# Nineteen 16-column products without a reader, and one of 512 columns fewer, in an encoder layer on one core

## The chip, the core and the metric

The kernel runs on one core of one Trainium2 chip. The core has a matrix engine (TensorE; PE in the profile, PEld for its weight loads), VectorE (DVE), ScalarE (ACT), GpSimd (POOL) and SyncE (SP), each with an instruction queue of its own that is worked off in order. Data lies in SBUF, and products add up in eight banks of PSUM. The metric is the device time of one execution in microseconds, the median of several runs; lower is better.

## The reference

One layer of a bidirectional encoder, 512 tokens of 1024 channels, all in float32:

```
n = rms_norm(h); proj = n @ w_in
h = h + (gate_a * (s5(xa) @ w_proj_a) + gate_b * (sgu(zu, zv) @ w_proj_b)) @ w_out
hn = rms_norm(h); memn = rms_norm(mem)              # mem: 256 tokens
q = hn @ w_q; k = memn @ w_k; v = memn @ w_v        # 4 heads of 256
h = h + softmax(q k^T / 16) v @ w_xo
hn = rms_norm(h)
h = h + (silu(hn @ w_gate) * (hn @ w_up)) @ w_down   # 1024 -> 2816 -> 1024
out = rms_norm(h)
```

## The kernel before, in words

Each float32 operand is split into a high part, which is the value rounded to the matrix engine's fp32r type, and a low part, the rest. One float32 product is then three fp32r products that add up in PSUM: high by high, high by low, low by high. `mm3` (lines 420 to 426) issues these three; `product` (line 1296) does the same for one of the seven products of a Strassen-like scheme, 24 instructions of 256 columns each: two column blocks j, four k, three parts. A weight block is loaded by DMA, and ScalarE (`whi`, line 85) and VectorE (`wlo`, line 86) split it, two blocks ahead of its use.

The stages that matter here come in this order. **Keys**: `feat(w_k, ...)`, four calls over 256 columns, each into two PSUM banks pf of 256 columns, four groups of twelve products; the moving operand is mn, the normalised memory, and transposes (ptr, line 584) of the query input stand between them. **Values**: two calls of `tokm(w_v, ...)`, each into two banks pt of 512 columns. **Queries**: 14 calls of `product` with q tiles qx, qv and qq (256 columns). Then attention and its output product, whose last blocks of rows t = 0 to 3 (pt, 512 columns) each end in an addition to h, a row norm (ACT square, DVE, POOL power) and a scaling into xs (DVE, line 576). `turn_row(t)` turns xs by eight transposes (ptr, line 1722) into the feed-forward input fn.

**Feed-forward entry**: the list LEAD gives (unit, q) of the first sixteen calls of `product`: (0,1), (1,1), (0,2), (2,1), (1,2), (2,2) and so on. The first two read only the first two blocks of rows. **Units**: eleven column blocks of w_gate and w_up, seven products each; the last one (**the last job**) has two parts of the down product (dx, 512 columns) between its products 6, 7, 4 and 3. **Down**: seven products in 512 columns (dx, dq, dv), and the **last products** (line 2072 on): dv in 256 columns for the last block of rows, then the last norm.

What sets the order: the program is written in one order, and a scheduler with a time model of its own moves instructions of an engine against each other as long as data and buffers allow. An instruction given to `in_order` keeps its place in the written order among those given to it; `pinned[0]` switches that on for whole stretches. In `product`, only the first of the 24 instructions is pinned, and only while `pinned[0]` is set: in LEAD from the third call on. Buffers that another engine frees (PSUM banks by `bank` and `aux`) are waited for by semaphore.

At the fourth call of LEAD stands a product without a reader: `idle`, 512 columns (line 1864), into an `aux` bank that nothing reads.

Of the kernel before, what the change touches and what calls it, by code (L numbers as in the profile page):

```python
# [17 lines left out]
P = 128  # L18
# [34 lines left out]
def hybrid_layer_kernel(  # L53
# [8 lines left out]
    nc = tc.nc  # L62
# [31 lines left out]
    pinned, halved = [False], [None]  # L94
    in_order = tc.keep_in_program_order
# [300 lines left out]
    def next_w(*key):  # L396
        i = used_w[0]
        used_w[0] += 1
        assert len(plan[i][0]) == len(key) and plan[i][0][1:] == key[1:] and plan[i][0][0] is key[0]
        for j in range(i, min(i + FAR + 1, len(plan))):  # L400
            begin(j, i)
            if j - 1 >= len(tiles) and j - 1 <= i + SPLITS:
                split_w(j - 1)
        for j in range(len(tiles), min(i + SPLITS + 1, len(plan))):
            split_w(j)
        tile_, tiles[i] = tiles[i], None
        return tile_
# [10 lines left out]
    def split_w(j):  # L418
        tiles.append(plan[j][2]())

    def mm3(ps, a, b, start, stop, free=False, turn=False):

        for i, (x, y) in enumerate(((0, 0), (0, 1), (1, 0))):
            m = nc.tensor.matmul(ps, a[x], b[y], start=start and i == 0, stop=stop and i == 2, skip_group_check=free)  # L424
            if turn:
                in_order(m)
# [38 lines left out]
    def tokm(w, c0, act, nk, evac, ntok=NT, last=2, kpt=2, cut=None, t0=0):  # L465


        toks = range(t0, t0 + ntok)
        ps = {t: bank(f"pt{t - t0}") for t in toks}
        nw = nk // kpt  # L470
        held = []
        full = slice(0, 512)
        for wi in range(nw):
            hi, lo = next_w(w, wi * kpt, kpt, c0, 512)
            held.append((wi, hi, lo))
            if wi < nw - last:
                todo, held = held, []
                for t in toks:
                    end = cut is not None and t == ntok - 1 and wi == nw - last - 1
                    tok_block(ps[t], t, todo, act, kpt, full, wi == 0, end)  # L480
                    if end:
                        cut(None, ps[t])
                tick(1.3 * ntok)
        for t in toks:
            if cut is not None and t == ntok - 1:
                for i in range(2):
                    p = aux("pcut", (P, 256))
                    tok_block(p, t, held, act, kpt, slice(256 * i, 256 * i + 256), True, True)
# [18 lines left out]
    def later(n, fn):  # L507

        side["later"].append((side["now"] + n, fn))
# [7 lines left out]
    def tick(us=5.2):  # L517

        side["now"] += us / 5.2
        run_due()  # L520
        side["credit"] = min(side["credit"] + us * side["rate"], us)
        while side["credit"] > 0.0 and side["gen"] is not None:
            try:
                used = next(side["gen"])
            except StopIteration:
                side["gen"] = None
                return
            if used is None:
                side["credit"] = 0.0
                return  # L530
            side["credit"] -= used
# [631 lines left out]
    held = [(3,) + next_w(w_in, 6, 2, OFF_V, 512)]  # L1163
# [92 lines left out]
    for h in range(H):  # L1256
        ps = bank("psv")
# [12 lines left out]
    K0, K1, T0, T1 = slice(0, 4), slice(4, 8), slice(0, 256), slice(256, 512)  # L1270
# [26 lines left out]
    def product(ps, u, q, start, ops):  # L1297

        hi, lo = next_w(u[0], u[1], q)
        for j in range(2):  # L1300
            cs = slice(j * P, (j + 1) * P)
            for k in range(4):
                a = (hi[:, k, cs], lo[:, k, cs])
                b = (ops[q][0][:, k, :], ops[q][1][:, k, :])
                for i, (x, y) in enumerate(((0, 0), (0, 1), (1, 0))):
                    m = nc.tensor.matmul(ps[:, j, :], a[x], b[y], start=start and j == k == i == 0,  # L1306
                                         stop=k == 3 and i == 2, skip_group_check=True)
                    if pinned[0] and j == k == i == 0:
                        in_order(m)
        tick(2.7)  # L1310

# [47 lines left out]
    for q, ts in ((5, T1), (6, T0)):  # L1359
        for i in range(2):  # L1360
            k = slice(2 * i, 2 * i + 2)
# [158 lines left out]
    def v_evac(half):  # L1520
        def f(t, ps):
            if not vts:
                vt = ap_.tile([P, 2, NM, D], F32R, tag="vt", name="vt", bufs=1)
                vts.extend((vt[:, 0], vt[:, 1]))
            vt_hi, vt_lo = vts
            cs = slice(half * 512, half * 512 + 512)
            split(vt_hi[:, t, cs], vt_lo[:, t, cs], ps)
        return f
# [18 lines left out]

    sums = []
    later(2, token_sums)
    for c0 in range(0, D, 256):  # L1550
        feat(w_k, c0, mn, KD, k_evac, n=M)
    for half in range(2):
        tokm(w_v, half * 512, mn, KD, v_evac(half), ntok=NM)


    qs = {}
# [108 lines left out]
    fn_hi, fn_lo = token_slot("fn", AWAY)  # L1665
# [3 lines left out]
    ps = {t: bank(f"pt{t}") for t in range(NT)}  # L1669
    held = []  # L1670
# [55 lines left out]
    held, ps = [], {}  # L1726
# [46 lines left out]
    ops = {1: fn_q(K0, T0), 2: fn_q(K1, T0), 7: fn_q(K0, T1), 4: fn_q(K1, T1)}  # L1773
# [25 lines left out]
    def put(u, f, ts, src):  # L1799
        dst = pair[:, :, ts] if u is UNITS[0] else acts(u[1] // 512, f)[:, :, ts]  # L1800
        if f == 0 if u is UNITS[0] else u[0] is w_gate:
            pin(nc.scalar.activation(dst, src, AF.Silu))
        else:
            pin(nc.vector.tensor_tensor(dst, dst, src, ALU.mult))
# [55 lines left out]
              9: third_sums, 10: lambda: make_op(3, 4, a12), 11: begun_sums[4]}  # L1860
    for i, (n, q) in enumerate(LEAD):
        pinned[0] = i >= 2
        if i == 3:
            in_order(nc.tensor.matmul(aux("idle", (P, 2, 256)), ops[1][0][:, 0, 0:P], fn_hi[:, 4:6, T0], start=True, stop=True))
        lead_product(n, q, beside.get(i, lambda: None))
        if i == 1:
            fifth_part(2)
# [6 lines left out]
    made, last_job = {}, []  # L1874
# [37 lines left out]
    def down_product(ps, q, start, chunks=range(CHUNKS)):  # L1912
        for c in chunks:
            rows_product(ps, q, c, next_w(w_down, q, c), (0, 1), slice(0, 512), start and c == 0, c == CHUNKS - 1,
                         chunks[0] == c > 0)

    for i, u in list(enumerate(UNITS))[2:]:
        final = i == len(UNITS) - 1
        x, v = begun
        q = unit_bank("pq")  # L1920
        product(q, u, 5, True, ops)
        if final:
            last_job.append(u)
            make_tokens(1, 0)
        product(x, u, 6, False, ops)
        u2 = copied(x, "u2")
        if not final:
            begun = unit_start(UNITS[i + 1])
        else:
            dx = [bank(f"dx{t}") for t in range(2)]  # L1930
            down_product(dx, 1, True, range(1))
        product(x, u, 7, False, ops)
        u3 = copied(x, "u3")
        if not final:
            unit_second(UNITS[i + 1], begun[1])
        else:
            down_product(dx, 1, True, range(1, 2))
        V.tensor_tensor(u3, q, u3, ALU.subtract)
        put(u, 1, T1, u3)
        product(x, u, 4, False, ops)  # L1940
        put(u, 0, T1, x)
        if u[0] is w_up:
            a_, b_ = (acts(u[1] // 512, f)[:, :, T1] for f in (0, 1))
            V.tensor_tensor(a_, a_, b_, ALU.subtract)
        product(q, u, 3, False, ops)
        V.tensor_tensor(u2, q, u2, ALU.subtract)
        put(u, 1, T0, u2)


    g_o = gain(final_norm_g, "g_o")  # L1950
# [28 lines left out]
    def finish(t):  # L1979
        half = 1 - early[t]  # L1980
        sum_sq(hss[:, 2, t, half:half + 1], h[:, t, HALF[half]])
        r = inv_root(t, hss[:, 2, t, half:half + 1])
        if pinned[0]:
            write(t, r)
        else:
            later(0.5, lambda: write(t, r))
# [69 lines left out]
    held = []  # L2056
# [12 lines left out]
    pinned[0] = True  # L2069
    in_order(nc.vector.tensor_tensor(h[:, 2, HALF[1]], h[:, 2, HALF[1]], dq[0], ALU.add))  # L2070
    finish(2)
    for i in range(2):
        for c, ops_ in held:
            rows_product({1: last[i]}, 4, c, ops_, (1,), slice(256 * i, 256 * i + 256), False, c == CHUNKS - 1, True)
        finish_last(i)
# [34 lines left out]
```

## Time and profile before

| | |
|---|---|
| time, median of 3 runs | 861.56 us (859.37 to 863.41) |
| profiled execution | 860.82 us, its span 859.0 us |
| PE | 851.8 us busy, 5736 products |
| PEld | 763.4 us |
| DVE / ACT / POOL | 666.8 / 469.0 / 91.9 us |
| granted TensorE clock | 0.998 |

In a row of a group or a timeline `px<-fn,whi` is the output tile and what it is made of, 128x256 its partitions and columns, x24 the number of such instructions. In the chain of waits a row is the start of a stretch in us from the span's start, its length, engine, tile, line and count; a stretch lasts until the next takes over, so length by count is the time from one product to the next. A row of a table of windows gives the window, its length, PE's busy time with the number of products, the granted clock, the share of the DMA engines and GB/s.

### The profile page before, as it was taken

To read this page: it belongs to the slowest core of one execution; us is meant where nothing else is said; L and a number is where in the kernel's file an instruction comes from. 1 tells how busy PE (TensorE), PEld (TensorE's weight loads), DVE (VectorE), ACT (ScalarE), POOL (GpSimd) and SP (SyncE) were. 2 spreads that over 40 slices of the span, in tenths; PEclk is the share of its full clock that TensorE was granted. 3 is DMA by queue.
4 is the path that set the end of the run, shared out by engine and by line. 5 is a ranking of instruction groups with operands and counts; after the bars stand their busy time and mean duration, and the time that the engine had idled before them with its cause. 6 is when DMAs were issued, how large, how long until landed. Compare 5 with 4: busy or idle time off the path is not lost.

```text
span 859.0 us, 14713 instructions
## 1 busy us (share of the span) xinstructions
PE 851.8 (99%) x5736; PEld 763.4 (89%) x5736; DVE 666.8 (78%) x1082; ACT 469.0 (55%) x703; POOL 91.9 (11%) x123
## 2 busy tenths in 40 slices
PE   9999999999999999999999999999999999999997
PEld 7888888888889988889899888999999999988886
DVE  7898888899646768669758755888877768899876
ACT  7834953244445544457556554655545555656674
POOL 0002101211021110210010101002111111000000
PEclk9999999999999999999999999999999999999999
DMA  9779666888575798947686845489999898366564
GB/s 273 212 243 246 144 172 161 227 204 209 143 222 153 241 301 269 301 150 243 205 270 169 198 136 138 146 229 229 226 225 238 217 247 186 101 190 208 196 187 157
DMA packets 119480, 176.37 MB, mean 205 GB/s; under 512 B 9665, under 2 KB 83537, under 8 KB 119250
## 3 DMA queue, kind: packets, MB, share of 16 engines
q1 hardware_dynamic: 96946, 144.18, 51.1%
q0 software_dynamic: 22176, 30.64, 22.2%
q8 instruction: 45, 0.74, 0.3%
q10 hardware_dynamic: 288, 0.61, 0.2%
q14 instruction: 25, 0.20, 0.1%
HBM read 166.52 MB, written 52.92 MB: 255 GB/s over the span
## 4 chain that ended last, share of the span: by engine, by line
PE 96%; DMA 2%; DVE 1%; issue 0%; ACT 0%; SPq 0%; ACTq 0%
PE pf L424 24%; PE pt L424 17%; PE px L1306 14%; PE pq L1306 7%; PE dx L424 5%; PE dq L424 4%; PE pv L1306 3%; PE bx L1306 3%; PE qx L1306 3%; PE dv L424 2%; PE pz L1013 2%; PE qv L1306 1%; PE po L424 1%; PE psc L424 1%; PE py L1070 1%; PE qq L1306 1%
## 5 line engine op out<-in xcount | busy, mean ns | idle before, releaser
L85 ACT CAST whi<-wraw 128x1024 fp32r<-128x1024 f32 (+1 forms) x145 | 149.5, 1031 | 166.7 <-PE pf L424 58.9
L86 DVE TENSOR_TENSOR wlo<-wraw,whi 128x1024 fp32r<-128x1024 f32 (+1 forms) x145 | 173.1, 1195 | 56.8 <-ACT whi L85 56.3
L424 PE MATMUL pf<-xn,whi 128*128 128x512 f32 x448 | 139.4, 392 | 0.0
L424 PEld LDWEIGHTS pf<-xn,whi 128*128 128x128 f32 x448 | 83.4, 188 | 16.9 <-issue 0.2
L1306 PE MATMUL px<-fn,whi 128*128 128x256 f32 x512 | 89.0, 277 | 0.0
L424 PE MATMUL pf<-xn,wlo 128*128 128x512 f32 x224 | 87.7, 392 | 0.0
L1306 PEld LDWEIGHTS px<-fn,whi 128*128 128x128 f32 x512 | 77.5, 188 | 0.2
L1306 PE MATMUL px<-fn,wlo 128*128 128x256 f32 x256 | 70.8, 277 | 0.0
L86 DVE TENSOR_TENSOR wlo<-b,whi 128x1024 fp32r<-128x1024 f32 x39 | 47.7, 1222 | 25.0 <-ACT whi L85 25.0
L85 ACT CAST whi<-b 128x1024 fp32r<-128x1024 f32 x39 | 41.1, 1053 | 42.5 <-PE px L1306 25.1
L1306 PE MATMUL pq<-s,whi 128*128 128x256 f32 x352 | 60.5, 276 | 0.0
L1306 PEld LDWEIGHTS pq<-s,whi 128*128 128x128 f32 x352 | 53.0, 188 | 0.0
L424 PEld LDWEIGHTS pf<-xn,wlo 128*128 128x128 f32 x224 | 42.0, 188 | 8.9 <-issue 0.2
L1306 PE MATMUL pq<-s,wlo 128*128 128x256 f32 x176 | 48.5, 276 | 0.0
L86 DVE TENSOR_TENSOR wlo<-t,whi 128x1024 fp32r<-128x1024 f32 x30 | 36.7, 1224 | 14.9 <-ACT whi L85 14.9
L85 ACT CAST whi<-t 128x1024 fp32r<-128x1024 f32 x30 | 31.6, 1053 | 30.4 <-DVE t L206 11.5
L1306 PEld LDWEIGHTS px<-fn,wlo 128*128 128x128 f32 x256 | 48.1, 188 | 0.0
L424 PE MATMUL pt<-whi,xn 128*128 128x512 f32 x128 | 43.3, 403 | 0.0
L424 PE MATMUL dx<-whi,s 128*128 128x512 f32 x132 | 41.4, 390 | 0.0
L424 PE MATMUL dq<-whi,s 128*128 128x512 f32 x122 | 38.1, 389 | 0.0
L1306 PEld LDWEIGHTS pq<-s,wlo 128*128 128x128 f32 x176 | 33.0, 188 | 0.0
L1306 PE MATMUL pv<-fn,whi 128*128 128x256 f32 x176 | 30.8, 277 | 0.0
(465 smaller groups left out, 2180.5 us busy)
## 6 DMA issues: line engine op xcount, KB each, us to landing
wraw<-in_w_in_dram SPq DMA_DIRECT2D x34, 512.0 KB, 4.9
dsum<-in_w_down_dram SPq DMA_DIRECT2D x20, 512.0 KB, 5.9
wraw<-dsum SPq DMA_DIRECT2D x20, 512.0 KB, 4.0
b<-in_w_gate_dram SPq DMA_DIRECT2D x15, 512.0 KB, 4.7
wraw<-in_w_down_dram SPq DMA_DIRECT2D x15, 512.0 KB, 4.0
b<-in_w_up_dram SPq DMA_DIRECT2D x14, 512.0 KB, 5.4
dsum<-in_w_down_dram POOLq DMA_DIRECT2D x10, 512.0 KB, 7.3
dsum<-dsum POOLq DMA_DIRECT2D x10, 512.0 KB, 6.9
```

Of the source, the lines that this page charges most:

```text
L85: hi = nc.scalar.copy(dst_hi, src)
L86: lo = nc.vector.tensor_tensor(dst_lo, src, dst_hi.bitcast(F32), ALU.subtract)
L424: m = nc.tensor.matmul(ps, a[x], b[y], start=start and i == 0, stop=stop and i == 2, skip_group_check=free)
L1013: nc.tensor.matmul(ps[:, g, :], wt[:, g, :], u[:, o * GO + g, :], start=True, stop=True)
L1070: in_order(nc.tensor.matmul(ps[64 * j:64 * j + 64, :, :, h, :].rearrange("p q d c -> p d q c"), a, b, start=k == ks[0], stop=k == ks[2], t ...
L1306: m = nc.tensor.matmul(ps[:, j, :], a[x], b[y], start=start and j == k == i == 0, stop=k == 3 and i == 2, skip_group_check=True)
```

## The change

`little` issues one product of 16 columns with 16 columns of weights, taken from the operands of the product that follows, with start and stop set; nothing reads what it leaves. In a group that starts fresh it writes into the corner of that group's own bank, which the group's first product then overwrites; otherwise it goes into an `aux` bank called idle. A switch `small[0]` turns it on in `mm3` (for a group's first product) and in `product` (once per call). It is on for the keys (8 small products, one for each pf bank) and the values (4), for the first, second and fourth call of LEAD (3), and for products 7, 4 and 3 of the last job (3), off for the dx part between; one more stands ahead of the last products. The 512-column idle product of the fourth LEAD call goes. While `small[0]` is on, the first instruction of `product` is pinned too, and so is the small product there.

```
+    def little(ps, a, b, fixed=False):
+        m = nc.tensor.matmul(ps[0:16, 0:16], a[:, 0:16], b[:, 0:16], start=True, stop=True, skip_group_check=True)
+        return in_order(m) if pinned[0] or fixed else m
+
     def mm3(ps, a, b, start, stop, free=False, turn=False):
 
+        if small[0] and start:
+            little(ps, a[0], b[0])
...
                 b = (ops[q][0][:, k, :], ops[q][1][:, k, :])
+                if small[0] and j == k == 0:
+                    little(ps[:, 0, :] if start else aux("idle"), a[0], b[0], True)
...
-                    if pinned[0] and j == k == i == 0:
+                    if (pinned[0] or small[0]) and j == k == i == 0:
                         in_order(m)
...
+    small[0] = True
     for c0 in range(0, D, 256):
         feat(w_k, c0, mn, KD, k_evac, n=M)
     for half in range(2):
         tokm(w_v, half * 512, mn, KD, v_evac(half), ntok=NM)
+    small[0] = False
...
     for i, (n, q) in enumerate(LEAD):
         pinned[0] = i >= 2
-        if i == 3:
-            in_order(nc.tensor.matmul(aux("idle", (P, 2, 256)), ops[1][0][:, 0, 0:P], fn_hi[:, 4:6, T0], start=True, stop=True))
+        small[0] = i in (0, 1, 3)
         lead_product(n, q, beside.get(i, lambda: None))
...
             down_product(dx, 1, True, range(1))
+            small[0] = True
         product(x, u, 7, False, ops)
...
+            small[0] = False
             down_product(dx, 1, True, range(1, 2))
+            small[0] = True
         V.tensor_tensor(u3, q, u3, ALU.subtract)
...
+    small[0] = False
...
     finish(2)
+    little(aux("idle"), held[0][1][0][:, 0], made[4, held[0][0] // 2][0][:, 0])
     for i in range(2):
         for c, ops_ in held:
             rows_product({1: last[i]}, 4, c, ops_, (1,), slice(256 * i, 256 * i + 256), False, c == CHUNKS - 1, True)
```

The new lines shift the rest: `mm3` is line 432 in the changed kernel, `product` 1316, the transposes of `turn_row` 1734; a small product of `mm3` or `product` has line 424.

The order of PE's instructions at the feed-forward entry, before (with what an instruction waits for in brackets; pt_5567 is the output product's bank of the last block of rows, s_5478 the first unit's weights):

```order
L424 MATMUL pt_5567<-s_5454,ot_hi 128x512 x2
L424 MATMUL pt_5567<-s_5454,ot_lo 128x512
L1306 MATMUL px<-fn,s_5478 128x256 [waits Activation_49]
L1306 MATMUL px<-fn,s_5478 128x256 [waits DVE_49]
L1306 MATMUL px<-fn,s_5478 128x256 x22
L1722 MATMUL ptr<-ident,xs 128x128 [waits DVE_49,PE_49]
L1722 MATMUL ptr<-ident,xs 128x128 x3
L1722 MATMUL ptr<-ident,xs 128x128 [waits DVE_49,PE_49]
L1722 MATMUL ptr<-ident,xs 128x128 x3
L1306 MATMUL px<-fn,whi 128x256 x2
```

and in the changed kernel:

```order
L432 MATMUL pt_5579<-s_5466,ot_lo 128x512
L1734 MATMUL ptr<-ident,xs 128x128 [waits DVE_49,Activation_49]
L1734 MATMUL ptr<-ident,xs 128x128 x3
L1734 MATMUL ptr<-ident,xs 128x128 [waits DVE_49,Activation_49]
L1734 MATMUL ptr<-ident,xs 128x128 x3
L424 MATMUL px<-fn,s_5490 16x16
L1316 MATMUL px<-fn,s_5490 128x256 [waits Activation_49]
L1316 MATMUL px<-fn,s_5490 128x256 x23
L1734 MATMUL ptr<-ident,xs 128x128 [waits DVE_49,PE_49]
L1734 MATMUL ptr<-ident,xs 128x128 x3
L1734 MATMUL ptr<-ident,xs 128x128 [waits DVE_49,Activation_49]
L1734 MATMUL ptr<-ident,xs 128x128 x3
```

The eight transposes of the third block of rows stood behind the first call's 24 products and now stand ahead of them, behind the last pt product; those of the fourth block, which stood in two groups of four inside the second call, now stand ahead of that call.

In the last job, behind the first dx part, the changed kernel has:

```order
L432 MATMUL dx_8088<-wlo,s_8052 128x512
L432 MATMUL dx_8088<-whi,s_8052 128x512
L424 MATMUL idle<-fn,whi 16x16
L1316 MATMUL px<-fn,whi 128x256 [waits Activation_49]
L1316 MATMUL px<-fn,whi 128x256
L1316 MATMUL px<-fn,wlo 128x256
```

One row of 16x16 stands between dx and px, where px followed dx before; nothing else moves there on PE.

More of the change, by code (lines that the diff above doesn't have):

```diff
@@ L419, in split_w, with little @@
         tiles.append(plan[j][2]())
+    small = [False]
+    def little(ps, a, b, fixed=False):
+        m = nc.tensor.matmul(ps[0:16, 0:16], a[:, 0:16], b[:, 0:16], start=True, stop=True, skip_group_check=True)
+        return in_order(m) if pinned[0] or fixed else m
     def mm3(ps, a, b, start, stop, free=False, turn=False):
+        if small[0] and start:
+            little(ps, a[0], b[0])
         for i, (x, y) in enumerate(((0, 0), (0, 1), (1, 0))):
@@ L1304, in product @@
                 b = (ops[q][0][:, k, :], ops[q][1][:, k, :])
+                if small[0] and j == k == 0:
+                    little(ps[:, 0, :] if start else aux("idle"), a[0], b[0], True)
                 for i, (x, y) in enumerate(((0, 0), (0, 1), (1, 0))):
@@ L1307, in product @@
                                          stop=k == 3 and i == 2, skip_group_check=True)
-                    if pinned[0] and j == k == i == 0:
+                    if (pinned[0] or small[0]) and j == k == i == 0:
                         in_order(m)
@@ L1549, in hybrid_layer_kernel @@
     later(2, token_sums)
+    small[0] = True
     for c0 in range(0, D, 256):
@@ L1553, in hybrid_layer_kernel @@
         tokm(w_v, half * 512, mn, KD, v_evac(half), ntok=NM)
+    small[0] = False
     qs = {}
@@ L1862, in hybrid_layer_kernel @@
         pinned[0] = i >= 2
-        if i == 3:
-            in_order(nc.tensor.matmul(aux("idle", (P, 2, 256)), ops[1][0][:, 0, 0:P], fn_hi[:, 4:6, T0], start=True, stop=True))
+        small[0] = i in (0, 1, 3)
         lead_product(n, q, beside.get(i, lambda: None))
@@ L1931, in hybrid_layer_kernel @@
             down_product(dx, 1, True, range(1))
+            small[0] = True
         product(x, u, 7, False, ops)
@@ L1936, in hybrid_layer_kernel @@
         else:
+            small[0] = False
             down_product(dx, 1, True, range(1, 2))
+            small[0] = True
         V.tensor_tensor(u3, q, u3, ALU.subtract)
@@ L1947, in hybrid_layer_kernel @@
         put(u, 1, T0, u2)
+    small[0] = False
     g_o = gain(final_norm_g, "g_o")
@@ L2071, in hybrid_layer_kernel @@
     finish(2)
+    little(aux("idle"), held[0][1][0][:, 0], made[4, held[0][0] // 2][0][:, 0])
     for i in range(2):
```

## The prediction

> **What bounds the kernel now.** I read the page first, its engine shares and the chain that ended last.
>
> ```profile
> span 859.0 us, 14713 instructions
> PE 851.8 (99%) x5736; PEld 763.4 (89%) x5736; DVE 666.8 (78%) x1082; ACT 469.0 (55%) x703; POOL 91.9 (11%) x123
> PEclk9999999999999999999999999999999999999999
> PE 96%; DMA 2%; DVE 1%; issue 0%; ACT 0%; SPq 0%; ACTq 0%
> ```
>
> TensorE (PE) is never out of work, its clock is never reduced, and the chain lies on it for 96% of the span. So nothing is to be had from waits; what counts is how long one product holds the engine, from its start to the start of the next. The busy column can't say that, since products overlap (a product of 256 columns is listed with 276 ns or more). I took it from the chain of waits shown stretch by stretch: start, length, tile, count. A stretch's length over its count is the time per product.
>
> Here are the stretches that follow each other from the keys to the query products; pf and pt hold keys (256 columns) and values (512 columns), ptr are transposes, qx and qq the query products (256 columns).
>
> ```profile
> 377.85 0.87 PE ptr L584 x8
> 388.53 3.42 PE pf L424 x30
> 393.20 10.96 PE pf L424 x93
> 404.15 22.40 PE pt L424 x96
> 426.55 2.74 PE qx L1306 x24
> 458.76 2.72 PE qx L1306 x24
> 461.94 0.44 PE ppt L1595 x4
> 300.27 11.80 PE pf L424 x52
> ```
>
> The query products take 2.72/24 = 113.3 ns each, the keys from 393.20 on 10.96/93 = 117.8. The values take 22.40/96 = 233.3 ns, while 512 columns elsewhere (the row at 300.27) take 11.80/52 = 226.9. So one and the same product comes in a **short** pace (113 and 227 ns) and a **long** one (118 and 233), with no wait in either. The long one, once there, stays: 93 keys and 96 values in a row.
>
> The same reading for the entry of the feed-forward, its last job and the last products:
>
> ```profile
> 530.32 5.49 PE pt L424 x24
> 535.80 2.83 PE px L1306 x24
> 538.63 0.87 PE ptr L1722 x8
> 539.50 2.60 PE px L1306 x22
> 543.33 2.71 PE pv L1306 x23
> 546.04 0.23 PE idle L1864
> 546.28 2.74 PE px L1306 x24
> 742.28 2.83 PE px L1306 x24
> 745.11 2.72 PE dx L424 x12
> 747.83 2.83 PE px L1306 x24
> 750.65 2.83 PE pq L1306 x24
> 849.80 3.60 PE dv L424 x30
> ```
>
> All the rows of 256 columns are long here (2.83/24 = 118, 3.60/30 = 120), except that the product without a reader of 512 columns (idle, 0.23 us) turned the long pace into the short one: 2.71/23 = 118 before it, 2.74/24 = 114 behind it. The short pace then lasted to the end of the units, 1701 products in 192.5 us = 113.2 ns:
>
> ```profile
> 546.50:739.00 192.50, 192.50 (x1701) 1.00 0.83 206
> ```
>
> The places with the long pace are the ones where the change sets its small products.
>
> **The change part by part.** Everything is counted against the profiled execution (860.82 us, span 859.0), which lies 0.74 under the median of the runs, 861.56.
>
> *What can be won.* Keys: 10.96 - 93 x 0.1133 = 0.42. Values: 22.40 - 96 x 0.2269 = 0.62. Entry, three rows: 2.83 - 2.72, 2.60 - 22 x 0.1133 and 2.71 - 23 x 0.1133, 0.11 + 0.11 + 0.10 = 0.32. Last job, three rows: 3 x 0.11 = 0.33. Last products: 3.60 - 30 x 0.1133 = 0.20. Together 1.89. The 512-column product that goes is 0.23 more, so 2.12 if every one of these places becomes short. If a small product does nothing to the pace, 0.23 is left.
>
> *What nineteen small products cost.* No fp32r product of 16 columns by 16 is in the trace. The nearest rows:
>
> ```profile
> 114.18 1.73 PE pz L1013 x16
> 60.45 0.10 PE pk L946 x15
> 140.30 0.16 PE pgb L1216
> ```
>
> A pz has 64 columns and takes 108 ns; a transpose has 128 and takes 0.87/8 = 109. Half the columns save nothing, so the 128-column weight load of the next product sets the pace there, and the product behind a small one has such a load. pk has weights of 16 columns and is followed by its like: 7 ns each. pgb, 16 columns with 128 columns of weights, holds 0.16. The bounds are thus 19 x 0.007 = 0.1 and 19 x 0.16 = 3.0. I take 0.109, since the weight load behind the small product is the full one: 19 x 0.109 = **2.07**, all of it on the chain. That alone eats what can be won.
>
> The Trainium skill, "TensorE: Matmul & The Clock Gate", section "Wait — 56ns, not 53.3ns?", gives about 25 ns as the smallest distance between two starts, however few the columns; by it the nineteen would cost an estimated 0.48 us and the whole sum below would be 0.24. The trace does not bear the figure out: pk stands at 7, below it, and pz at 108, far above.
>
> *What the pin does at the entry.* The change also ties the first product of a call to the written order wherever small products are on. The rows of the order show it: the eight transposes of the third block of rows stood behind the first 24 px products, now they stand ahead of them, right behind the last pt product. They read xs, which VectorE makes here:
>
> ```profile
> 535.41 0.39 PE L424 MATMUL pt<-s,ot_lo 128*128 128x512 f32 x1
> 535.64 2.99 PE L1306 MATMUL px<-fn,s 128*128 128x256 f32 x24
> 533.74 0.68 DVE L1494 TENSOR_TENSOR h<-h,pt 128x512 f32<-128x512 f32 x1
> 536.44 1.41 DVE L576 SCALAR_TENSOR_TENSOR xs<-h,r,g_f 128x512 f32<-128x512 f32 x2
> L576 DVE SCALAR_TENSOR_TENSOR xs<-h,r,g_f x4: 743/745/752, 536.4 to 539.5; 128x512 f32<-128x512 f32 x4
> ```
>
> PE is free for the next instruction at 535.64. The halves of xs are ready at 536.44 + 0.74 = 537.18 and at 536.44 + 1.41 = 537.85. The scaling hangs on h, which waits for the pt products, so it can't come earlier. Today the 24 px products (2.83 us) cover this wait; afterwards nothing does, for the px products, and all else on the in-order engine, are queued behind the transposes. From 535.64 to 537.18, a tenth for the first weight load (a transpose's share above), 4 x 0.109 of transposes to 537.73, then until 537.85 and a tenth again: 1.65 + 0.23 = **1.9** us of standing. Bounds: 1.5 if a weight load is taken ahead of the wait, 2.1 if each wait costs another tenth. Below nothing it can't be: the same eight transposes are issued either way. The transposes of the fourth block now stand behind the px products; their xs is ready at 539.5 + 0.75 = 540.25, and PE gets there at 535.64 + 0.87 + 1.9 + 0.11 + 2.72 = 541.24. No second wait.
>
> *At nothing:* the transposes that move by a few products among the keys (their xs lies ready by then) and the new places of some token sums on VectorE and ScalarE in the last job; the weight blocks there are split two blocks ahead, and a block is twelve products (the dx rows of 2.72), so 5.4 us of PE work cover moves by one instruction of 1.2. Without that cover such a move would cost up to 1.2.
>
> ```profile
> L86 DVE TENSOR_TENSOR wlo<-wraw,whi 128x1024 fp32r<-128x1024 f32 (+1 forms) x145 | 173.1, 1195 | 56.8 <-ACT whi L85 56.3
> ```
>
> Sum: 2.07 - 2.12 + 1.9 = **+1.85**. 860.82 + 1.85 = 862.7 in the profiled execution, and with 0.74 to the median **863.4**.
>
> **The rivals.**
>
> *Values short, queries long.* In every place where 512 columns in the short pace lead straight into 256 columns, these are long: 530.32 (228.8 ns each, transient included) into 535.80, 745.11 (226.7) into 747.83. Out of long 512 columns came short ones: 404.15 into 426.55, and the idle product. If the small products make the values short, the query products, which get none, could become long until the transposes at 461.94 (ppt): 461.94 - 426.55 = 35.4 us are 312 products, 312 x (117.8 - 113.3) = 1.4. Then 863.4 + 1.4 = **864.8**. Against it: the rule rests on few places.
>
> *Cheap small products.* If the weight load of the product behind is taken while the one ahead still runs, a small one could cost near pk's 7 ns, say 30: 19 x 0.03 = 0.57, the sum is 0.57 - 2.12 + 1.9 = 0.35 and the time **861.9**. For it speaks pk; against it that weights of 128 columns are what follows, as with pz. One load does run ahead, as the idle product shows:
>
> ```profile
> L1864 PEld LDWEIGHTS idle<-fn x1: 188/188/188, 545.8 to 545.8; 128*128 128x128 f32 x1
> L1864 PE MATMUL idle<-fn x1: 399/399/399, 545.9 to 545.9; 128*128 128x512 f32 x1
> ```
>
> The same page, section "Step-by-step: what each phase is for", says that weight loads are pulled ahead of running products into a background buffer. The trace agrees for one load (the idle product's is taken at 545.8, the product starts at 545.9); whether two fit, which is what this case needs, no run here shows.
>
> *No cure.* A 16-column product is not the 512-column one that is known to turn the pace. Without effect the change is 2.07 - 0.23 + 1.9 = 3.74 longer: **865.3**.
>
> *The units in the long pace* (the other side). What settles the pace of the 1701 unit products is now the small product at their head. Streams that start behind a run of transposes settled short (388.53, 3.42/30 = 114) or long (393.20). Should the units start long, they cost 1701 x 4.5 ns = 7.7: 863.4 + 7.7 = **871.1**. It decides as soon as the first 24 px products behind the third small one take 2.83 instead of 2.74. For it speaks that the known cure is taken out at exactly this place.
>
> *No wait at the entry*, should xs be ready when PE comes: 863.4 - 1.9 = **861.5**. The rows above speak against it.
>
> **How the numbers follow.** Forecast 0.38; queries long 0.20; cheap small products 0.14; no cure 0.12; units long 0.12; no wait 0.04. Likeliest: **863.4**. Half a per cent, 4.3 us, is what this kernel's runs (859.37 to 863.41) can tell from no change: 857.3 and 865.9 are the marks. Slower than that are the units (0.12), half of no cure (0.06) and a small part of the queries (0.04): 0.22. Faster needs cheap products, no wait and more: 0.03. Within: 0.75. Range: the lower end is the case without a wait less about one for the spread of the runs, 860.5; above it reaches over queries long and no cure with spread, 867.0. Outside are the units and tails, about 0.18.
>
> **What would show it.** Right: a gap of PE of 1.5 to 2 us ahead of the first ptr at L1734, ended by xs on VectorE; keys at 113 and values at 227 ns; about 0.11 us added for each 16-column product (a start of the following product some 110 ns behind it). Wrong: ptr without a gap; the small products at under 50 ns; px behind the third one at 118. The whole is wrong if the time is under 860.5 or the units are long.

## The result

| | before | changed |
|---|---|---|
| median | 861.55 us (859.37 to 864.23, 8 runs) | 870.3 us (862.84 to 872.35, 8 runs) |
| ratio | | 1.0088, 95% interval 1.0067 to 1.0108 |
| profiled execution | 860.82 us, span 859.0 | 863.58 us, span 861.8 |

The changed kernel is slower by 0.9%. The forecast, 863.4 us with a range to 867.0, missed it; the rival called "the units in the long pace", with 871.1 us and a chance of 0.12, is what came in most executions.

Its executions fall in two groups that have nothing to do with the granted clock (0.996 to 1.000 in both). Of all seventeen, with the two repetitions below (e1 and e12), four took 862.84 to 864.65 us, one 866.49, and twelve 869.34 to 873.15 with a median of 870.5. The profiled execution beside the result is one of the lower group, so its trace alone would not explain the median. A later one (e12) caught the upper group. Two executions ran at a reduced clock (1064.11 us at 0.753 in e4; 1435.82 us at 0.558, the kernel before beside e13 and e14) and are left out of what is compared.

### The profile page after: what moved, and what is told of

It reads as the page before. It is cut to its first block, busy times and chain, and to the rows that moved or that the text cites. A ratio compares the mean times of both kernels' runs of the same rounds, so it can differ in the third digit from the quotient of the medians.

```text
span 861.8 us, 14749 instructions
## 1 busy us (share of the span) xinstructions
PE 852.3 (99%) x5754; PEld 762.1 (88%) x5754; DVE 666.9 (77%) x1082; ACT 468.2 (54%) x703; POOL 91.7 (11%) x123
## 4 chain that ended last, share of the span: by engine, by line
PE 94%; DVE 3%; DMA 1%; issue 1%; ACT 1%; POOL 0%; SPq 0%; POOLq 0%; ACTq 0%
PE pf L432 24%; PE pt L432 14%; PE px L1316 14%; PE pq L1316 7%; PE dx L432 5%; PE dq L432 5%; PE pv L1316 3%; PE bx L1316 3%; PE qx L1316 3%; PE dv L432 2%; PE pz L1021 2%; PE qv L1316 1%; PE po L432 1%; PE psc L432 1%; PE py L1078 1%; PE qq L1316 1%
## 5 line engine op out<-in xcount | busy, mean ns | idle before, releaser
L1316 PE MATMUL px<-s,whi 128*128 128x256 f32 x176 | 30.7, 276 | 0.0
```

## The profile after

The page of the changed kernel, execution of 863.58 us:

```profile
span 861.8 us, 14749 instructions
PE 852.3 (99%) x5754; PEld 762.1 (88%) x5754; DVE 666.9 (77%) x1082; ACT 468.2 (54%) x703; POOL 91.7 (11%) x123
PE 94%; DVE 3%; DMA 1%; issue 1%; ACT 1%; POOL 0%; SPq 0%; POOLq 0%; ACTq 0%
```

TensorE is as full as before. Its chain of waits (start in us, length, engine, tile, line, count), then the wait for VectorE (sum, number, longest) and the units (window, length, PE busy with its products, clock):

```profile
376.43 0.87 PE ptr L592 x8
391.94 1.48 PE pf L432 x12
393.43 2.94 PE pf L432 x24
426.63 2.74 PE qx L1316 x24
539.54 2.85 PE px L1316 x24
543.27 2.93 PE px L1316 x24
546.20 2.83 PE pv L1316 x24
549.02 0.01 PE px L424
549.03 2.84 PE px L1316 x24
745.15 2.84 PE px L1316 x24
753.59 2.93 PE pq L1316 x24
852.45 3.70 PE dv L432 x30
...
PE ptr L1734 <- DVE xs L584: 1.8, 1, 1.8
...
550.00:738.00 188.00, 188.00 (x1661) 1.00 0.85 210
```

How to read the row at 549.02: the small product itself shows as 0.01 us, and the 24 products behind it carry its price. Without one, 24 products take 2.72 in the short pace and 2.83 in the long one; behind a small product they take 2.84 and 2.93. So 2.84 at 549.03 is short with 0.11 of price, and 2.93 at 543.27 is long. The units here run at 188.00/1661 = 113.2 ns: short, as before the change.

Now the same places in the execution of 869.79 us (e12, the same kernel):

```profile
span 868.0 us, 14749 instructions
...
376.59 0.87 PE ptr L592 x8
412.95 13.15 PE pt L432 x57
426.10 2.75 PE qx L1316 x24
542.00 2.84 PE px L1316 x24
544.84 2.72 PE pv L1316 x24
547.56 0.01 PE px L424
547.57 2.93 PE px L1316 x24
751.12 2.84 PE px L1316 x24
858.68 3.69 PE dv L432 x30
...
550.00:738.00 188.00, 188.00 (x1599) 1.00 0.84 208
```

Two rows have changed places. Ahead of the third small product the 24 pv products take 2.72 (short) where they took 2.83 (long), and behind it the units are at 188.00/1599 = 117.6 ns where they were at 113.2. The values, the row at 412.95, run at 13.15/57 = 230.7 ns, with the price of the small product ahead of them in it; the account below comes back to them. Cut at the starts of rows shown here and, for the kernel before, in the prediction, the three spans add up like this:

| from ... to, us | before | changed, 863.58 | changed, 869.79 |
|---|---|---|---|
| start ... transposes ahead of the keys | 377.85 | 376.43 | 376.59 |
| ... first query product (keys and values) | 48.70 | 50.20 | 49.51 |
| ... first product behind the third small product (idle before) | 119.73 | 122.40 | 121.47 |
| ... px behind the first dx of the last job (the units) | 196.00 | 196.12 | 203.55 |
| ... first dv | 107.52 | 107.30 | 107.56 |
| ... end of the span | 9.20 | 9.35 | 9.32 |

The step between the two groups is in one row: 203.55 - 196.12 = 7.4 us in the units. The first row moves by 1.4 us although the change touches nothing there.

## The experiments

Each is timed beside the kernel before on the same chip, whose median was 860.98 to 862.04 us; ratios are to that. "Upper" and "lower" mean executions near 870 and near 864.

**e1, the changed kernel unchanged.**

> The changed kernel once more, nothing altered, to see an execution of the usual length. Theory U (the pace of the units is left to chance behind the third small product): times fall into two groups, near 863 and near 870; an execution of 870 has the 1700 products between 549 and 742 us at 117.8 ns instead of 113.2, which is 7.7 us, and all else within 1 us of the profile in hand. Rival D (spread over many places): in an execution of 870 the units stand at 113 and the 7 us lie in keys, values, queries (312 x 4.5 ns = 1.4) and the down products (423 x 6.5 ns = 2.7). Rival W (waits): PE stands idle for several us somewhere.

869.74 us (863.39 to 873.15, 8 runs), ratio 1.0092 (1.0061 to 1.0123). Two lower, one at 866.49, five upper. The result repeats, and so do the groups.

**e2, the third small product exchanged for the old idle product of 512 columns.**

```
-        small[0] = i in (0, 1, 3)
+        if i == 3:
+            in_order(<the idle product of 512 columns>)
+        small[0] = i in (0, 1)
```

> The changed kernel with one thing undone: the third small product of the entry (fourth call of LEAD) is the 512-column product without a reader again; the other eighteen small products and the pins stay. Theory U: one group of times only, 863.5 + 0.1, the units at 113 ns in every execution. Rival D and W: no difference to the changed kernel, median near 870.

864.74 us (862.56 to 865.72, 10 runs), ratio 1.0035 (1.002 to 1.005): one group, no execution near 870. The trace has the units at 113:

```profile
546.81 2.72 PE pv L1316 x24
549.53 0.23 PE idle L1876
...
550.00:738.00 188.00, 188.00 (x1661) 1.00 0.86 211
```

With the other eighteen small products and the pins in place, this one exchange takes 870 down to 864.7. What costs the 0.6% is what stands at the head of the units.

**e3, the kernel before without its idle product and with nothing in its place.**

```
-        if i == 3:
-            in_order(<the idle product of 512 columns>)
```

> The kernel before with the 512-column product without a reader taken out and nothing put in its place. Theory U: the long pace of the second call's products (118) goes on through the units, 1704 x 4.6 ns = 7.8 us longer less 0.23, near 869 in every execution. Rival D: 0.2 us faster than before, 861.3.

869.39 us (868.04 to 870.68, 4 runs), ratio 1.0096 (1.0067 to 1.0125):

```profile
546.02 2.71 PE pv L1306 x23
...
550.00:738.00 188.00, 188.00 (x1599) 1.00 0.84 208
```

Before the idle product stood the long pace (2.71/23 = 118), and without it the pace stays long to the end of the units, 1599 products in the window like in e12. The removal alone costs as much as the whole change.

**e4, the kernel before with only its idle product made 16 columns.**

```
-            in_order(nc.tensor.matmul(aux("idle", (P, 2, 256)), ops[1][0][:, 0, 0:P], fn_hi[:, 4:6, T0], ...))
+            in_order(nc.tensor.matmul(aux("idle", (P, 2, 256))[0:16, 0, 0:16], ops[1][0][:, 0, 0:16], fn_hi[:, 4, 0:16], ...))
```

> The kernel before with only one thing of the change: the 512-column product without a reader becomes one of 16 columns at the same place. Theory U: two groups of times, near 861.4 and near 869, the second one in most executions, with no stall and no other small product in it. Rival D: 861.4 in all. If 16 columns never turn the pace: 869 in all, as without any product there.

862.48 us, the median of nine executions (eight from 859.36 to 862.86, one at 869.84), ratio 1.0019 (0.9995 to 1.0043). In the trace the 23 pv ahead of it are long, and the units behind it short:

```profile
542.77 2.71 PE pv L1306 x23
...
550.00:738.00 188.00, 188.00 (x1661) 1.00 0.86 211
```

So the same 16 columns that fail in the changed kernel mostly do the idle product's work in the order of the kernel before: eight executions of nine, where the expectation had most of them long. Something ahead of it may decide; e5 tries that.

**e5, the changed kernel with the entry in its old order:** no small products and no pins in the first two calls of LEAD.

```
-        small[0] = i in (0, 1, 3)
+        small[0] = i == 3
```

> The changed kernel without the small products of the first two calls of LEAD, and with nothing pinned there: the transposes of the third block of rows come behind the product into px again, as before the change. The small product ahead of the third call that is pinned (the one in place of the idle product) and those of keys, values, last job and last products stay. Theory (the pace of the units is settled by chance where the third small product stands, whatever comes ahead of it): still two groups, the lower one near 863.4 - 1.9 (no wait for xs) - 0.2 (two small products fewer) = 861.3, the upper one 7 above it at about 868.3, and more executions in the upper group than in the lower. Rival (it is the changed order at the entry that tips the pace, since the kernel before with only the third product made small had one of nine there): nearly one group at 861.3 to 862, with at most one in eight near 868.

861.47 us (860.17 to 863.56, 10 runs), ratio 1.0 (0.9983 to 1.0016), none near 868. The theory (chance, whatever stands ahead) falls and its rival holds: the entry decides, that is the changed order together with the wait and the two small products that come with it. And all the rest of the change (small products in keys, values, last job and last products, and the third) comes out at no difference.

```profile
543.30 2.71 PE pv L1316 x23
...
550.00:738.00 188.00, 188.00 (x1662) 1.00 0.85 211
```

**e6, the changed kernel with a 512-column product in the seventh unit,** behind 1008 of the 1704 products.

```
         product(q, u, 5, True, ops)
+        if i == 6:
+            in_order(<a product without a reader, 512 columns>)
```

> The changed kernel, with a product without a reader of 512 columns added in the seventh unit, behind some 1008 of the 1704 products of the units. Theory (in its upper group all products of the units take 118 ns in place of 113, and a product of 512 columns settles the pace anew): the upper group comes down from 870.5 to about 863.6 + 1008 x 4.5 ns + 0.23 = 868.3, the lower stays at 863.8; in a trace of an upper execution the products are at 118 up to the added one and at 113 behind it. Rival (the 7 us of the upper group lie somewhere else, or the pace is not settled by such a product in the middle of the units): groups as in the changed kernel, 863.6 and 870.7.

869.46 us (863.94 to 872.05, 9 runs), ratio 1.0087 (1.0064 to 1.011). The upper executions (eight, median 869.7) came down by 0.8 us from 870.5, less than the 2.2 expected; the spread within the group is as large as that. The trace of an upper one (872.05 us) settles the matter where the times don't; its units, cut as in the table, take 753.64 - 552.82 = 200.8 us in place of 203.55:

```profile
550.09 2.72 PE pv L1316 x24
...
553.00:671.00 118.00, 118.00 (x1004) 1.00 0.81 202
671.64 0.23 PE idle L1934
672.00:750.00 78.00, 78.00 (x690) 1.00 0.81 202
```

Short ahead of the small product (2.72), long behind it (118.00/1004 = 117.5), and short again behind the 512 columns (78.00/690 = 113.0).

**e7, the kernel before with only the pins at the entry:** no small product, the idle product kept.

```
-                    if pinned[0] and j == k == i == 0:
+                    if (pinned[0] or tied[0]) and j == k == i == 0:
...
+        tied[0] = i < 2
```

> The kernel before with the first product of the first two calls of LEAD tied into the order written out, nothing else: no small product anywhere, and the idle product of 512 columns kept. So the transposes of the third block of rows stand ahead of the products into px, as in the changed kernel. Theory (PE then waits 1.8 us for xs of VectorE, and the idle product keeps the units short): 861.3 + 1.9 = 863.2, and one group. Rival (the wait is absorbed by a later one): 861.3. Rival (the order at the entry alone makes the units long): most executions near 870.

862.44 us (860.59 to 867.09, 10 runs), ratio 1.0017 (0.9998 to 1.0036), that is 1.5 us with bounds of -0.2 and 3.1; 1.9 lies within, and so does nothing. No execution is near 870, so the order alone, with the idle product kept, does not make the units long. The profiled execution is the slowest, 867.09 us; its units are short all the same (187.00/1653 = 113.1), and its query products are long. The trace has the stall, and it has the stretch ahead of the idle product in the short pace, where it is long in the kernel before:

```profile
548.72 2.72 PE pv L1308 x24
...
553.00:740.00 187.00, 187.00 (x1653) 1.00 0.86 211
...
PE ptr L1724 <- DVE xs L578: 1.8, 1, 1.8
```

**e8, the idle product of the kernel before 256 columns wide.**

```
-            in_order(nc.tensor.matmul(aux("idle", (P, 2, 256)), ..., fn_hi[:, 4:6, T0], ...))
+            in_order(nc.tensor.matmul(aux("idle", (P, 2, 256))[:, 0], ..., fn_hi[:, 4, T0], ...))
```

> The kernel before with its idle product 256 columns wide in place of 512. Theory (only a product that differs in length from the stream of 256 columns settles the pace): it is one more product of the same kind, so the pace is what it would be with nothing there, and the time is that of the kernel without the idle product, 869.4 (units at 118). Rival (any product without a reader does it): 861.2.

869.06 us (867.7 to 870.28, 4 runs), ratio 1.0079 (1.0051 to 1.0107). One more product like those around it does nothing; the units stay long:

```profile
547.54 0.12 PE idle L1864
547.66 2.83 PE px L1306 x24
```

At this point the traces suggested a rule. Wherever a small product stood between two stretches of 256 columns, a short stretch was followed by a long one, in 11 cases of 11; a long one was followed by a short one in 9 of 14. These are few places, seen again in several traces: the short ones lie at one place in the keys, one in the last job and the third small product. In the old order of the entry the stretch ahead of the idle product was long in every trace (before, e3, e4, e5, e8); in the changed order it was long in two (the changed kernel and e1) and short in three (e2, e6, e7).

**e9, e7 with the idle product made 16 columns** (the two edits of e4 and e7 together, nothing else).

> The kernel before with the entry in the changed order (the first product of the first two calls of LEAD tied) and its idle product 16 columns in place of 512; no other small product. Theory (a 16-column product behind a stretch of 256-column products in the short pace leaves the long one, 11 of 11 in the traces so far, and behind a stretch in the long pace mostly the short one, 9 of 14; in the changed order without small products the stretch ahead of the third was short): nearly all executions have the units long, 862.4 + 7.5 = 869 to 870, and the trace shows the 48 products ahead at 113 and the 1704 behind at 118. Rival (the small product draws the pace anew whatever is ahead of it, and the third draws the short one as in the kernel before with the third alone): most near 862.3.

869.51 us (861.78 to 871.34, 10 runs), ratio 1.0068 (1.004 to 1.0095): six upper, four lower. Not "nearly all" upper. The pace ahead is not always short in this order: in the one profiled execution, a lower one (864.09 us), it was long, and was turned.

```profile
546.86 2.83 PE pv L1308 x24
...
550.00:738.00 188.00, 188.00 (x1661) 1.00 0.85 210
```

But pins and the 16-column product together, without any other small product, make the two groups: by their times, long units in six executions of ten, where the pins alone have none of ten (e7) and the 16 columns alone one of nine (e4). Whether it is the moved transposes or the wait that comes with them, no run separates.

**e10, the changed kernel with a 16-column product in the seventh unit** (as e6, 16 columns).

> The changed kernel with a product of 16 columns added in the seventh unit, behind 1008 of the 1704 products. Theory (it turns the pace over): an execution with short units becomes long for the last 696, 863.6 + 696 x 4.6 ns + 0.1 = 866.9, one with long units short, 870.6 - 3.2 + 0.1 = 867.5, so that the two groups meet at about 867, where the changed kernel has no execution between 866.5 and 869.3; the trace shows one pace ahead of it and the other behind. Rival (it leaves the pace as it is): groups at 863.7 and 870.7. Rival (it settles the short pace): 863.7 and 867.5.

870.14 us (867.38, 869.76, 870.52, 871.17), ratio 1.0093 (1.0073 to 1.0114). The trace shows it turn the pace from long to short (118.00/1004 = 117.5, then 77.00/682 = 112.9):

```profile
552.00:670.00 118.00, 118.00 (x1004) 1.00 0.82 203
671.00:748.00 77.00, 77.00 (x682) 1.00 0.81 201
```

The times did not gather at 867, so as a test by times it failed: four are few, and the profiled execution took 3.2 us more than e12 between the first query product and the third small product, 1.4 us of it in the query products, which ran long.

**e11, a candidate: the kernel before with a 512-column product without a reader behind the first 24 query products.** Some rows of the attention change places behind it.

```
     qq_ = unit_bank("qq")
+    nc.tensor.matmul(qq_, hops[1][0][:, 0, 0:P], hn_hi[:, 4:6, T0], start=True, stop=True)
     query_product(qq_, 0, 5, True)
```

> The kernel before with a product without a reader of 512 columns behind the first 24 of the 312 query products (some rows of the attention change places behind it). The traces so far have the queries short in seven and long in three. Theory (such a product leaves the short pace): the trace shows the 288 behind it at 113; 0.23 is paid always and 288 x 4.6 ns = 1.32 saved in a third of the executions, so 861.3 + 0.23 - 0.4 = 861.1, no difference that can be told, with fewer executions above 862.5. Rival (behind a short stretch it can leave the long one): slower by up to 1.5, 862.8.

861.58 us (859.51 to 863.41, 12 runs), ratio 0.9994 (0.998 to 1.0007): no difference that can be told. The place did turn short, which pays 0.23 to save up to 1.3 in some executions:

```profile
427.33 2.83 PE qx L1306 x24
...
430.39 2.74 PE qq L1306 x24
```

**e12, the changed kernel once more, for its trace.**

> The changed kernel once more, for its trace. Theory: when the execution is near 870, the 1704 products of the units are at 118 and the 48 ahead of the third small product at 113; when it is near 864, the other way round, 113 and 118, as in its two traces so far.

869.79 us, and its rows are those shown above: 2.72 ahead of the small product, 117.6 ns behind it. As expected.

**e13, the pace ahead of the third small product set on purpose:** the changed kernel with a 512-column product one call earlier.

```
+        if i == 2:
+            in_order(<a product without a reader, 512 columns>)
         small[0] = i in (0, 1, 3)
```

> The changed kernel with a product without a reader of 512 columns one call (24 products) ahead of its third small product. Theory (the 512 columns leave the stretch short, and a 16-column product behind a short stretch leaves the long pace): all executions in the upper group, 870.7 + 0.2 = 870.9, none near 863.8; the trace shows 24 products at 113, then 1704 at 118. Rival (the small product draws a pace whatever is ahead of it): two groups as in the changed kernel, about a third of the executions near 863.8.

872.56 us (872.36 to 873.14, 4 runs), ratio 1.0135 (1.0114 to 1.0156): all upper, none lower. They lie 1.7 above the expected 870.9; in the profiled one the query products were long, which is 1.4 of it.

```profile
547.85 2.73 PE pv L1316 x24
...
553.00:740.00 187.00, 187.00 (x1590) 1.00 0.84 209
```

Set to short (2.73), the stretch is followed by long units (187.00/1590 = 117.6). No execution is in the lower group. Four of four would also come by luck in a quarter of cases if each had the chance of twelve in seventeen; with the four of e14, which has the same 512 columns there, it is eight of eight and 0.06. The weight lies on the traces: in all five with a short stretch ahead of the third small product (e6, e10, e12, this one and e14) the products behind it were long.

**e14, the same with another small product 24 products behind the third.**

```
-        small[0] = i in (0, 1, 3)
+        small[0] = i in (0, 1, 3, 4)
```

> The same with one more 16-column product at the fifth call of LEAD, 24 products behind the third small one. Theory (it turns the long pace that the third left into the short one): all executions in the lower group, 863.6 + 0.23 + 0.11 + 24 x 4.6 ns = 864.0; the trace shows 24 at 113, 24 at 118 and 1680 at 113. Rival (a pace drawn anew): two groups. Rival (a small product behind a long stretch leaves it long, as at 397.6 in the keys): all near 871.

871.79 us (871.31 to 873.49, 4 runs), ratio 1.0128 (1.0106 to 1.015): all upper, as the last rival had it. The second small product did not turn the long pace back:

```profile
551.42 2.93 PE px L1316 x24
...
556.00:740.00 184.00, 184.00 (x1564) 1.00 0.85 212
```

The units stay at 184.00/1564 = 117.6. So the half of the rule that reads "long becomes short" falls as a rule. Counted over all traces, short was followed by long in 23 cases of 23, long by short in 15 of 25. Nine of the ten that stayed long are one place in the keys, seen in nine traces (36 products that themselves began behind a small product); the tenth is the case just shown. At each place all traces with the same pace ahead agree, so these are not 48 independent cases. What sets a long stretch that turns apart from one that doesn't stays open, and so does what in the engine the two paces are.

The difference between the groups can be followed one call further back. With both small products at the entry, the 24 products of the first call were short and the second call long in three traces (the changed kernel, e1, e14), long and then short in four (e6, e10, e12, e13), and short both times in e2. So it is there already behind the wait for xs; what sets the pace of the first call is open.

## Why the prediction was wrong, point by point

**The step that failed** is the premise that a small product can only help or do nothing to the pace ("if a small product does nothing to the pace, 0.23 is left"), carried to the head of the units. There the idle product stood between long pv products and short unit products, its rows were quoted, and the forecast still had the units' pace at nothing and priced the removal as a gain of 0.23 us. e3 prices it: with nothing in its place the median is 8.1 us higher. What replaces it must leave the short pace whatever stands ahead. One product of 512 columns did that in every trace (e2, e6, e7, e11, e13, e14, behind long and short stretches alike), one of 256 did not (e8), and one of 16 did it behind some long stretches, and behind a short one never.

**The rival "units in the long pace"** had the place and the size right: 1701 x 4.5 ns = 7.7 against 7.4 between the two traces, 871.1 against 870.5 for the upper group. Only its chance was wrong, 0.12 against twelve executions of seventeen. The prediction gives no reason for a chance that small; its rows had streams behind transposes settling both ways. What it lacked was that the pin, in the prediction just a stall, also changes what stands ahead of the third small product. In the old order that stretch was long in all traces, and the 16 columns then did well (e5, and e4 in eight executions of nine). In the changed order it is often short, and then they leave the units long. Neither edit alone makes the units long in most executions; e9 shows that the pair does.

**The forecast's own case exists** as the lower group, four executions of 862.84 to 864.65 around its 863.4. That its profiled one lies so close is partly luck: ahead of the keys, where nothing was changed, it was 1.4 us shorter than the kernel before. Term by term:

- *The small product*, 0.109 each: right. 24 products behind one take 2.84 to 2.85 in place of 2.72 to 2.74, about 0.11. The rows of e12 show where it is paid:

```profile
547.39 0.17 PE L424 MATMUL px<-fn,whi 128*16 128x16 f32 x1
547.42 0.48 PE L1316 MATMUL px<-fn,whi 128*128 128x256 f32 x2
547.74 0.28 PE L1316 MATMUL px<-fn,wlo 128*128 128x256 f32 x1
...
547.40 0.30 PEld L1316 LDWEIGHTS px<-fn,whi 128*128 128x128 f32 x2
```

  The product behind the small one starts 27 ns after it, and the two at 547.42 then take 0.32 in place of 0.24. The load of 128 columns for the product behind starts only with the small product (547.40), and the load after that 109 ns later in the trace; so a small product costs the time of one more load, as the prediction argued from pz. That does away with the rival "cheap small products". The sign "a start of the following product some 110 ns behind it" holds only behind transposes; in a stream it is the product after that one that comes late. The Trainium skill ("TensorE: Matmul & The Clock Gate", "Wait — 56ns, not 53.3ns?") gives a floor of about 25 ns between two starts; the 27 ns lie near it, but they are not the price, and the estimate of 0.48 us for all nineteen falls (with it the prediction's sum would have been 0.26, not the 0.24 that it states).
- *The pin*, 1.9: right. The wait ahead of the transposes is 1.8 in the execution of 863.58 and in e7, and 1.5 in that of 869.79; the stage from queries to units grew by 1.7 (869.79) and 2.7 (863.58), where 1.9 + 0.33 - 0.32 - 0.23 = 1.7 were foreseen. The rival "no wait" is out. Of the 1 us more in the one trace, 0.6 came before the stall, from a late xs row among the last output products.
- *What can be won*, 1.89: about half of it came, in e12 an estimated 0.5 in keys and values, 0.2 at the entry and 0.2 in the last job. The last job runs short behind two of its small products (745.15) and long behind the third (753.59, 2.93), the last products stay long (3.70 for 30), the keys have both (391.94 short, 393.43 long), and in the changed kernel's traces the entry turns at one or two of its three rows. The values became neither short nor long: read start by start, they go 226, 229, 232 ns over and over, 229 on average, in place of 233 before and 227 foreseen. Keys and values together took 0.8 (e12) and 1.5 us more than before, where 1.31 of price less 1.04 of gain, 0.27, were foreseen. In traces of kernels that don't touch them this stretch takes from 48.70 to 50.80, and in five of these seven traces (e3, e7, e8, e9, e11) the values fall into the same 229 ns with no small product; so the one trace that the terms of 0.42 and 0.62 were read from could not carry them. e5, which has most of these small products and no stall, is level with the kernel before.
- *Queries long*: they are, in some executions with and without the change (36.8 us in e6 for what takes 35.4 in e12): in three of nine traces with small products in the values, and in four of seven without. So it belongs to the spread of the runs, and nothing here shows it as an effect of the change. Values at 227, the condition of this rival, were in no trace.

*No cure*, 865.3, came close to e2 (864.7) by its size, but by another path: e2 keeps the old cure. By the prediction's own rows its price was wrong: a product without effect at the head of the units leaves them in the long pace that stood ahead (2.71/23 = 118), as e3 and e8 show, so that 7.7 us belong on top, 873.0.

So the change costs about 2 us at the entry, nearly all of it the stall (the lower group's median of 863.5 against 861.5 in e5), nothing measurable by the rest of the small products, and 7.4 us more in about seven executions of ten by the units' pace.

## What to carry to other kernels

An instruction that no one reads may hold the time of everything behind it. When one is exchanged, compare the time per product ahead of it and behind it first, and multiply by the whole stream that follows, here 1704 products; a small price beside a large lever deserves more than a small chance. And before trusting a term read from one pair of stretches, see how much the same stretch moves between executions in which nothing was changed.

## What the runs showed that was not expected

- Two paces for the same gapless stream at a granted clock of 1.00: 113 and 118 ns for 256 columns, either of which holds for all of 1704 products; for 512 columns three, 227, 229 and 233.
- What is put between two stretches sets the pace of the second: behind one product of 512 columns it was short (e2, e6, e7, e11, e13, e14), behind one of 256 it went on as it was (e8), behind one of 16 it was long after a short stretch in 23 cases of 23 and short after a long one in 15 of 25, at few places seen in several traces. No run here shows the reason.
- Whole executions of one program can therefore differ by 7 us without a wait, a slower clock or a transfer behind it; a single trace of the changed kernel would have shown the harmless case.
